# A store held back by one small scaling: average pooling with kernel 4 on one core

## Chip, core and metric

The kernel runs on one core of one Trainium2 chip. The metric is device time in microseconds (us), the time of one launch; smaller is better. The engines that work are VectorE (DVE in the profile), ScalarE (ACT), and SyncE (SP), which issues loads. Data moves between HBM and SBUF on the core's 16 DMA engines.

## The reference

```python
x: (64, 256, 8192) float32, kernel_size = 4, stride = 4
for i in range(out_len):                       # 2048
    output[:, :, i] = np.mean(x[:, :, 4*i : 4*i+4], axis=2)
```

Every four neighbouring elements are averaged. 536.87 MB are read and 134.22 MB are written; there is hardly any arithmetic per byte.

## The kernel before, in words

The input is taken as one flat array and cut into 64 blocks of 128 partitions x 16384 elements (8.39 MB). Two blocks make a run, so there are 32 runs. One block becomes 128 x 4096 results, and one run is stored by a single DMA of 128 x 8192 results (4.19 MB).

There are two input buffers, `xt[0]` for the first and `xt[1]` for the second block of a run, and two output buffers `ot[0]` and `ot[1]`, which runs use in turn. The order of the work is written by hand with semaphores. The helper `take` (lines 60 to 61) waits on an engine until a semaphore has a value and takes that value off again. For each block of a run (function `pair`, lines 91 to 112):

- VectorE waits until the block has landed (`full[k]`, line 95). For the first block it then signals `landed` (line 97) and waits until the output buffer's last store is through (line 98).
- VectorE adds neighbours in two passes (`sums`, lines 75 to 81): 8192 sums in place (line 77), then 4096 sums into the output buffer (line 79).
- SyncE waits for that (`free`, line 101), signals ScalarE (`summed`, line 102) and issues the load of the same half of the next run into the buffer that has come free (line 103, through `load`, line 64). So a second block's load is issued when the second block of the run ahead of it has been summed.
- ScalarE multiplies the 4096 sums by 1/4 in place (line 106).

When both blocks are done, ScalarE issues the run's store on its own DMA queue (line 112). It first waits until its scaling is through (`scaled`, line 109) and, in lines 110 and 111, for `landed`: the first block of the *next* run must have landed. One `landed` is taken ahead of the loop (line 118), so that the count is right.

In the profile the loads run on queue q1 and ScalarE's stores on q10. Both queues use the same 16 DMA engines. A load is 8 packets of 65,536 bytes on each engine, a store 8 of 32,768, and each is followed by a small packet that raises the semaphore.

Thirty runs go through a loop of 15 passes (line 132) with the store on ScalarE. Run 30 (line 138) uses one `tensor_reduce` per block and is stored by SyncE; run 31 (lines 142 to 157) is done in smaller pieces. Both are written out behind the loop, and neither waits for `landed` before a store.

Of the kernel before, what the change touches and what calls it, by code (L numbers as in the profile page):

```python
# [1 line left out]

# [4 lines left out]


FULL = 16384
PAIR = 2  # L10
ROUND = 2 * PAIR

TAIL = (8192, 8192)


@with_exitstack
def kernel(
    ctx: ExitStack,
    tc: tile.TileContext,
    x: bass.AP,  # L20
    kernel_size: bass.AP,
    stride: bass.AP,
    out: bass.AP,
):
    nc = tc.nc
    K, S = int(kernel_size), int(stride)
    assert K == S == 4
    B, C, L = x.shape
    assert L % K == 0
    P = nc.NUM_PARTITIONS  # L30
    dt = x.dtype
    add, mult = mybir.AluOpType.add, mybir.AluOpType.mult

    M = FULL // K
    blocks = B * C * L // P // FULL
    runs = blocks // PAIR
    assert blocks * P * FULL == B * C * L and blocks % ROUND == 0 and sum(TAIL) == FULL

    xr = x.rearrange("b c l -> (b c l)").rearrange("(n p k m) -> n k p m", p=P, k=PAIR, m=FULL)
    orun = out.rearrange("b c l -> (b c l)").rearrange("(n p m) -> n p m", p=P, m=PAIR * M)  # L40


    xt0 = ctx.enter_context(nc.sbuf_tensor([P, FULL], dt))
    xt1 = ctx.enter_context(nc.sbuf_tensor([P, FULL], dt))
    ot0 = ctx.enter_context(nc.sbuf_tensor([P, PAIR * M], dt))
    ot1 = ctx.enter_context(nc.sbuf_tensor([P, PAIR * M], dt))
    xt, ot = [xt0, xt1], [ot0, ot1]


    full = [nc.alloc_semaphore(f"full{k}") for k in range(2)]  # L50
    piece = [nc.alloc_semaphore(f"piece{k}") for k in range(len(TAIL))]
    free = nc.alloc_semaphore("free")
    summed = nc.alloc_semaphore("summed")
    landed = nc.alloc_semaphore("landed")
    summed_last = nc.alloc_semaphore("summed_last")
    scaled = nc.alloc_semaphore("scaled")
    scaled_last = nc.alloc_semaphore("scaled_last")
    stored = [nc.alloc_semaphore(f"stored{k}") for k in range(2)]

    def take(engine, sem, n):  # L60
        engine.wait_ge(sem, n).then_inc(sem, -n)  # L61

    def load(n, k):
        d = nc.sync.dma_start(out=xt[k][:, :], in_=xr[n, k])
        d.then_inc(full[k], 16)
        return d

    for k in range(2):  # L70
        tc.no_tile_sem_insts.add(load(0, k).ins.name)
    tc.close()
    tc.compile()  # L73

    def sums(t, o):
        w = t.shape[1]
        nc.vector.tensor_tensor(out=t[:, : w // 2], in0=t[:, ::2], in1=t[:, 1::2], op=add)  # L77
        nc.vector.drain()
        return nc.vector.tensor_tensor(  # L79
            out=o, in0=t[:, : w // 2 : 2], in1=t[:, 1 : w // 2 : 2], op=add  # L80
        )

    def reduce(t, o):
        return nc.vector.tensor_reduce(  # L84
            out=o,
            in_=t.rearrange("p (m k) -> p m k", k=K),
            op=add,
            axis=mybir.AxisListType.X,
        )

    def pair(n, q, ahead, store):


        for k in range(PAIR):
            take(nc.vector, full[k], 16)
            if k == 0:
                nc.vector.sem_inc(landed, 1)
                take(nc.vector, stored[q], 16)
            add_up = sums if store is nc.scalar else reduce
            add_up(xt[k][:, :], ot[q][:, k * M : (k + 1) * M]).then_inc(free, 1)  # L100
            take(nc.sync, free, 1)
            nc.sync.sem_inc(summed, 1)
            ahead(k)
            o = ot[q][:, k * M : (k + 1) * M]
            take(nc.scalar, summed, 1)
            means = nc.scalar.mul(o, o, 1.0 / K)  # L106
        done = scaled if store is nc.scalar else scaled_last
        means.then_inc(done, 1)
        take(store, done, 1)
        if store is nc.scalar:  # L110
            take(store, landed, 1)
        store.dma_start(out=orun[n], in_=ot[q][:, :]).then_inc(stored[q], 16)


    zero = nc.const_aps.tensor(0.0, [P, 1], dt)
    nc.scalar.mul(ot[0][:, :1], zero, 1.0).then_inc(stored[0], 16)  # L116
    nc.scalar.sem_inc(stored[1], 16)
    take(nc.scalar, landed, 1)

    edges = [sum(TAIL[:i]) for i in range(len(TAIL) + 1)]  # L120
    pieces = list(zip(edges[:-1], edges[1:]))
    xe, oe = xr[runs - 1, 1], orun[runs - 1]

    def ahead_of_last(k):
        if k == 0:
            load(runs - 1, 0)
        else:
            for sem, (a, b) in zip(piece, pieces):
                nc.sync.dma_start(out=xt[1][:, a:b], in_=xe[:, a:b]).then_inc(sem, 16)

    engines = (mybir.EngineType.SP, mybir.EngineType.DVE, mybir.EngineType.Activation)
    with nc.Fori(0, (runs - 2) // 2, 1, engines=engines) as r:
        for q in range(2):
            n = r * 2 + q
            pair(n, q, lambda k: load(n + 1, k), nc.scalar)


    pair(runs - 2, 0, ahead_of_last, nc.sync)

    take(nc.vector, stored[1], 16)
    take(nc.vector, full[0], 16)
    sums(xt[0][:, :], ot[1][:, :M]).then_inc(summed_last, 1)
    for k, (sem, (a, b)) in enumerate(zip(piece, pieces)):
        take(nc.vector, sem, 16)
        sums(xt[1][:, a:b], ot[1][:, M + a // K : M + b // K]).then_inc(summed_last, 1)
        if k == 0:
            take(nc.scalar, summed_last, 1)
            nc.scalar.mul(ot[1][:, :M], ot[1][:, :M], 1.0 / K)  # L150
        o = ot[1][:, M + a // K : M + b // K]
        take(nc.scalar, summed_last, 1)
        nc.scalar.mul(o, o, 1.0 / K).then_inc(scaled, 1)  # L153
        take(nc.scalar, scaled, 1)
        c = 0 if k == 0 else M + a // K
        d = M + b // K
        nc.scalar.dma_start(out=oe[:, c:d], in_=ot[1][:, c:d]).then_inc(stored[1], 16)
    take(nc.sync, stored[0], 16)
    take(nc.sync, stored[1], 16 * len(TAIL))


# [1 line left out]
_INS = ['x', 'kernel_size', 'stride']  # L163
_OUTS = [((64, 256, 2048), 'float32')]

_NUMBERS = {'kernel_size': 4, 'stride': 4}


# [26 lines left out]
```

## Time and profile before

| | us |
|---|---|
| runs shown: lowest, median, highest of 3 | 1569.22, 1570.84, 1572.13 |
| the profiled execution, its own time | 1570.5 |
| span of the profiled execution, first to last instruction | 1569.2 |
| VectorE busy | 848.0 |
| ScalarE busy | 233.1 |
| loads, median from issue to landing | 35.0 |
| ScalarE's stores, median from issue to landing | 33.4 |

The page of the profile gives for each engine the busy time, its share of the span and the count of instructions. The DMA line has one digit for each of 40 slices of the span: the busy share of the 16 DMA engines in tenths, 9 being 90% or more. A queue's row gives packets, megabytes, and the time its packets took as a share of 16 engines' span. In a table of windows each row is a stretch of time: its limits, its length, the busy time and count of DVE, ACT and POOL, the TensorE clock, the DMA share and GB/s. A packet is counted whole in the window in which it starts, so the DMA share of a short window can be a little over 1. In the timeline a row is start, duration, engine, line and operation; the brackets give how long the engine sat idle before it and what released it. A row that ends in "x3" joins three instructions, and its duration runs from the first to the last. Behind the views stand the trace's records of every single DMA packet, with start, duration, size and queue but not the number of the DMA engine.

### The profile page before, as it was taken

The numbers are of one execution on the slowest core, as the hardware profiler recorded it, in microseconds if no ns is written. First come the engines' busy times: TensorE is split into PE (matmuls) and PEld (weight loads), VectorE is DVE, ScalarE is ACT, GpSimd is POOL, SyncE is SP. The second block draws the span as 40 slices with busy tenths as digits, with TensorE's granted clock in tenths as the row PEclk, the third lists the DMA queues.
The fourth block names the chain that finished last, engine by engine and source line by source line (L and its number), as shares of the span: only waits on it lengthen the run. The fifth ranks groups of instructions, "written<-read, shape, count | busy, mean of one in ns | idle before, by whom it ended". The sixth has DMA issues, their size and how long they took to land. (4 is left out here: it accounts for less than half of the span.)

```text
span 1569.2 us, 1086 instructions
## 1 busy us (share of the span) xinstructions
DVE 848.0 (54%) x128; ACT 233.1 (15%) x67; POOL 0.2 (0%) x4
## 2 busy tenths in 40 slices
DVE  3645546545465464664646546465464664646666
ACT  1101011010110101101011010110101101011011
POOL 0000000000000000000000000000000000000000
DMA  9999999999999999999999999999999999999999
GB/s 428 412 430 438 431 438 441 416 441 428 449 426 431 431 436 418 434 440 429 429 423 417 432 428 428 417 426 434 436 441 423 419 426 435 426 424 424 434 398 388
DMA packets 14112, 671.09 MB, mean 428 GB/s; under 512 B 1568, under 2 KB 1568, under 8 KB 1568
## 3 DMA queue, kind: packets, MB, share of 16 engines
q1 hardware_dynamic: 9504, 541.07, 80.6%
q10 hardware_dynamic: 4608, 130.03, 19.2%
HBM read 536.87 MB, written 134.22 MB: 428 GB/s over the span
## 5 line engine op out<-in xcount | busy, mean ns | idle before, releaser
L77 DVE TENSOR_TENSOR xt<-xt 128x8192 f32<-128x8192 f32 (+1 forms) x63 | 539.1, 8557 | 685.6 <-DVEq L61 685.6
L106 ACT ACTIVATE ot<-ot 128x4096 f32<-128x4096 f32 x62 | 224.2, 3616 | 1300.8 <-ACTq L61 1300.8
L79 DVE TENSOR_TENSOR ot<-xt 128x4096 f32<-128x4096 f32 (+1 forms) x63 | 274.5, 4358 | 4.7
L84 DVE TENSOR_REDUCE ot<-xt 128x4096 f32<-128x16384 f32 x2 | 34.4, 17220 | 18.3 <-DVEq L61 18.3
L150 ACT ACTIVATE ot<-ot 128x4096 f32<-128x4096 f32 x1 | 3.6, 3617 | 12.8 <-ACTq L61 12.8
L153 ACT ACTIVATE ot<-ot 128x2048 f32<-128x2048 f32 x2 | 3.8, 1910 | 9.5 <-ACTq L61 9.5
L116 ACT ACT_TABLE_LOAD x1 | 1.3, 1283 | 2.4 <-PEq L73 2.4
L116 ACT ACTIVATE ot<-const-float32-0.0 128x1 f32<-128x1 f32 x1 | 0.2, 203 | 0.0
L176 POOL MEMSET const-bfloat16-1.0<- 128x1 bf16 x1 | 0.1, 102 | 0.0
L176 POOL MEMSET const-uint8-127<- 128x1 uint8 x1 | 0.1, 102 | 0.0
L176 POOL MEMSET const-float32-0.0<- 128x1 f32 x1 | 0.1, 99 | 0.2 <-issue 0.2
L176 POOL MEMSET const-float32-1.0<- 128x1 f32 x1 | 0.1, 99 | 0.0
## 6 DMA issues: line engine op xcount, KB each, us to landing
out_dram<-ot ACTq DMA_DIRECT2D x30, 4096.0 KB, 33.4
xt<-in_x_dram SPq DMA_DIRECT2D x2, 4096.0 KB, 18.4
out_dram<-ot SPq DMA_DIRECT2D x1, 4096.0 KB, 34.0
out_dram<-ot ACTq DMA_DIRECT2D x1, 3072.0 KB, 16.2
out_dram<-ot ACTq DMA_DIRECT2D x1, 1024.0 KB, 10.4
xt<-in_x_dram SPq DMA_DIRECT2D x63, 35.0
```

The costliest lines, as they stand in the source:

```text
L77: nc.vector.tensor_tensor(out=t[:, : w // 2], in0=t[:, ::2], in1=t[:, 1::2], op=add)
L79: return nc.vector.tensor_tensor(out=o, in0=t[:, : w // 2 : 2], in1=t[:, 1 : w // 2 : 2], op=add)
L84: return nc.vector.tensor_reduce(out=o, in_=t.rearrange("p (m k) -> p m k", k=K), op=add, axis=mybir.AxisListType.X,)
L106: means = nc.scalar.mul(o, o, 1.0 / K)
L116: nc.scalar.mul(ot[0][:, :1], zero, 1.0).then_inc(stored[0], 16)
L150: nc.scalar.mul(ot[1][:, :M], ot[1][:, :M], 1.0 / K)
L153: nc.scalar.mul(o, o, 1.0 / K).then_inc(scaled, 1)
L176: nc = _bacc.Bacc("TRN2", target_bir_lowering=False, num_devices=1)
```

## The change

ScalarE no longer scales the 4096 columns of a run's second block in one instruction. It scales the first 2656, waits for `landed`, then scales the last 1440 and issues the store. The wait for `landed` between the scaling and the store is gone, since it has moved ahead of the second scaling. This holds for the 30 runs of the loop. Loads, sums, the first block's scaling, run 30 and run 31 are as before.

```diff
+REST = 1440
...
             take(nc.scalar, summed, 1)
+            if k == 1 and store is nc.scalar:
+                nc.scalar.mul(o[:, :-REST], o[:, :-REST], 1.0 / K)
+                take(nc.scalar, landed, 1)
+                o = o[:, -REST:]
             means = nc.scalar.mul(o, o, 1.0 / K)
         done = scaled if store is nc.scalar else scaled_last
         means.then_inc(done, 1)
         take(store, done, 1)
-        if store is nc.scalar:
-            take(store, landed, 1)
         store.dma_start(out=orun[n], in_=ot[q][:, :]).then_inc(stored[q], 16)
```

## The prediction

> **What bounds the kernel now.** I read the page first, then the windows cut at the store issues, then the timeline of one run, then the records of single DMA packets in the trace. The page:
>
> ```profile
> span 1569.2 us, 1086 instructions
> DVE 848.0 (54%) x128; ACT 233.1 (15%) x67; POOL 0.2 (0%) x4
> DMA  9999999999999999999999999999999999999999
> q1 hardware_dynamic: 9504, 541.07, 80.6%
> q10 hardware_dynamic: 4608, 130.03, 19.2%
> ```
>
> VectorE is busy for 54% and ScalarE for 15%, while the packets of both queues fill 80.6 + 19.2 = 99.8% of the time of the 16 DMA engines. No engine is the bound: the kernel ends when the bytes are through, so a gain must come from DMA packets that take less time, and a loss from longer ones or from a queue that runs empty. The windows, one per run, from one store issue to the next (length first, GB/s last), show that runs are not alike:
>
> ```profile
> 61.60:111.89 50.29, 26.22 (x5) 7.23 (x2) 0.00 (x0) 1.00 0.99 417
> 111.89:160.33 48.44, 26.24 (x5) 7.23 (x2) 0.00 (x0) 1.00 1.00 433
> ...
> 549.37:598.05 48.68, 26.24 (x5) 7.23 (x2) 0.00 (x0) 1.00 1.01 435
> 598.05:647.07 49.02, 26.23 (x5) 7.23 (x2) 0.00 (x0) 1.00 1.00 424
> ...
> 990.26:1039.71 49.45, 26.24 (x5) 7.23 (x2) 0.00 (x0) 1.00 1.00 423
> ```
>
> VectorE and ScalarE do the same work in each (26.2 and 7.23 us), yet a run takes between 48.44 and 49.45 us. The 28 runs from 111.89 to 1479.92 take 1368.03, or 48.86 each: the first ten 48.62, the other eighteen 48.99.
>
> The packet records (start, duration, size, queue) say where this goes. A 65,536-byte load packet takes 2418 ns undisturbed, a 32,768-byte store packet 1213 ns. Per run an engine has 16, 8, and 3 of 9 ns for semaphores: 38.69 + 9.70 + 0.03 = 48.42 us, less about 0.1 for the 4 ns by which neighbours overlap: 48.3. All packets together exceed these durations by 16.6 us per engine: 0.6 before the first store, 1.2 in the first run, 0.4 in the next ten, 12.0 in the following eighteen, 0.4 just behind the last of these stores and 1.8 in the tail. Nearly all of it lies in load packets 1 to 7 us behind a store issue.
>
> Joining packets whose start is another's end (less 4 ns) gives each engine's sequence. With T the store issue, at a block's landing: the engine that landed last has started its next load packet 0.72 us before T, in every run, because the store is released by that landing. In the first ten of the 28 runs, this last engine alone pays, 0.07 to 0.48 us a run, 0.25 on average; in the first nine of them the other fifteen pay 0.003. So it falls further behind each time: from 1.3 us behind the foremost to 4. From some 4.7 us on (598 us) another thing comes in: all 16 engines stretch a packet together around T + 4 us, by about 1 us, in most of the eighteen runs. The lead then stays near 5 us, since the foremost engines find their next load not yet there.
>
> **The change, part by part.** The timeline around one store:
>
> ```profile
> 982.89 3.62 ACT L106 ACTIVATE ot<-ot 128x4096 f32<-128x4096 f32 x1 [24.89 <-ACTq L61]
> 982.98 49.80 SPq L64 DMA_DIRECT2D xt<-in_x_dram  x3
> 990.21 8.69 DVE L77 TENSOR_TENSOR xt<-xt 128x8192 f32<-128x8192 f32 x1 [7.54 <-DVEq L61]
> 990.26 0.34 ACTq L112 DMA_DIRECT2D out_dram<-ot  x1
> 998.98 4.43 DVE L79 TENSOR_TENSOR ot<-xt 128x4096 f32<-128x4096 f32 x1
> 1003.63 3.62 ACT L106 ACTIVATE ot<-ot 128x4096 f32<-128x4096 f32 x1 [17.12 <-ACTq L61]
> ```
>
> ScalarE finishes a run at 982.89 + 3.62 = 986.51 and waits for the landing until 990.2; the store goes out 0.05 us behind VectorE's start on the landed block.
>
> *Added instructions.* ScalarE's rows give 3.616 us for 4096 columns, 1.910 for 2048, 0.203 for one: 0.833 ns a column and 0.2 fixed. So 2656 columns take 2.42 us, 1440 take 1.40, together 0.2 more than the one instruction: 30 x 0.2 = 6 us of ScalarE in all, beside 1300 us idle; nothing.
>
> *The moved wait.* The first part ends at 982.89 + 2.42 = 985.3, 4.9 us ahead of the landing, so the landing still ends the wait last. Behind it now stand 1.40 us of scaling and the hand-over to the store (in the tail 1548.44 + 1.91 to the issue at 1550.46: 0.11). The store goes out some 1.5 us later, 30 times. Queued behind it on ScalarE is only the next run's first scaling, at 1003.63, 11.9 us behind the new issue; if that cover were gone, ScalarE would hand its results on late. The buffer of the store is wanted again two runs on, 2 x 48.86 = 97.7 us, and the store lands 33.4 us after its issue. SyncE's loads wait for VectorE alone: the next goes out 13.2 us behind the landing as before, and while the store is held back the engines work on the load issued at 982.98, 7.3 us ahead of it. So 1.5 us without a store are filled with load packets, and the later store costs no time by itself. If that load were not there, the price would be the whole 30 x 1.5 = 45 us.
>
> *What it moves.* A store comes between load packets of 2.42 us, so 1.5 us is more than half a packet. The last engine, 0.72 us into its packet at the issue before, will be 2.2 us into it. The trace has this position: in the first two of the 28 runs the fourteen foremost engines were 1.65 to 2.19 us past the end of the landed load, in the first packet of their next one, and paid 0.00. Engines 0.72 to 0.92 us into that same first packet paid 0.06 to 0.48; one at 1.15 paid 0.22, at 1.13 and 1.41 nothing. By these rows the last engine would stop paying. The cost of the new position is bounded by the nearest rows: from nothing (48.44 a run or a little less) to the stretch of the run at 990.26, for all runs (49.45). I take the end near nothing, since its rows have the same place in the same load, and not just the same distance. Then it does not fall behind, 4.7 us are not reached, and the common stretch stays away too.
>
> *Sum.* If all 28 runs took 48.44: 28 x (48.86 - 48.44) = 11.8. If they took the 48.62 of the first ten: 28 x 0.24 = 6.7. The first run, the start and the tail stay as they are; the store issued at 1479.92 lands by 1515, 54 us ahead of the end. The profiled execution took 1570.5 us for its span of 1569.2, as good as the median of 1570.84, so I go from 1570.5: 1558.7 to 1563.8. I take **1561**.
>
> Against the change speaks a row, then a rule. From issue to landing a store takes 33.4 us, all of which moves back. The Trainium skill, "DMA: Bandwidth & Descriptors", section "Rules for kernel authors", says to issue a DMA early and wait late, so that its fixed cost is overlapped; by it the hold is a loss. No store here is waited for within 64 us of its landing, so the trace gives the rule little to act on.
>
> **The rivals.**
> *The last engine falls behind for a reason other than the store's position* (it may simply be the slower one), or something else stretches the packets from 598 us on, such as what is read there. Then the later store is hidden beside loads and nothing moves: 1570.5, give or take 3. For it: what the stretch is made of is not in the trace, and the runs at 647 and 1039 have little of it with the same lead. Against it: the engines paying, and the onset at 4.7 us of lead, go with position.
> *The later store meets the engines worse* and the common stretch starts in the first runs. It is decided by where the foremost engines stand when the first store packet enters, at T + 4 before and about T + 5.5 after; if the stretch belongs to stores entering with 4 us of spread, it stays, and the later store also adds its packets to the next load. All 28 runs at 48.99 give 28 x 0.13 = 3.7 more, 1574; all at 49.45 give 28 x 0.59 = 16.5, 1587. For it: all 16 engines stretched in the first run already, with 0.5 us of spread, so spread is not the only condition.
> *The hold is exposed*, the rule above as a mechanism of this kernel: the foremost engines run out of loads during it and idle, 30 x 1.5 = 45, 1615. Against it: the load is issued 7.3 us ahead.
> *The last engine still pays but the lead grows more slowly*, because the second load of a run lands earlier by up to one store packet (1.2 us) and its successor is issued earlier: the late runs come later; 1565 to 1567.
> That the change does not do what it says is excluded by the listing of ScalarE's instructions: 2656 and 1440 columns stand in the loop, the store behind them.
>
> **How the numbers follow.** Forecast 0.50 (1556 to 1566); slower growth 0.08; nothing moves 0.17; worse meeting 0.23; exposed hold 0.02. A measurement of this kernel can tell about 0.2% (3.1 us) from no change. Faster: 0.50 + 0.08 = 0.58; same 0.17; slower 0.23 + 0.02 = 0.25. The likeliest one's own range is 1556 to 1566. The range that should hold 8 in 10 starts at 1555, a little under the sum with 48.3 us a run, and reaches to 1577, past no change and the milder half of the worse meeting; outside stay the common stretch in full and the exposed hold.
>
> **What would show it.** In the changed profile: the store issue 1.5 us behind VectorE's start on the landed block; runs of 48.4 to 48.6 us through to the end, also beyond 598; the page's DMA share still 99% with more GB/s; in the packet records, fewer load packets over 2418 ns behind the store issues and a last engine that stays within 2 or 3 us of the foremost. Wrong would be the step on position, if runs lengthen again although the issue has moved; wrong would be the step on cover, if DMA shares drop below 0.98 in these windows.

## The result and the profile after

The changed kernel takes **1552.85 us** (median of 4, 1552.55 to 1553.13) against 1570.82 for the kernel before on the same chip (median of 4, 1569.22 to 1572.13): ratio 0.9886, interval 0.9869 to 0.9903, so 18 us less. Its profiled execution took 1552.82 us, with a span of 1551.5. The page after:

```profile
span 1551.5 us, 1116 instructions
DVE 847.9 (55%) x128; ACT 239.2 (15%) x97; POOL 0.2 (0%) x4
q1 hardware_dynamic: 9504, 541.07, 80.6%
q10 hardware_dynamic: 4608, 130.03, 19.4%
HBM read 536.87 MB, written 134.22 MB: 433 GB/s over the span
```

The DMA engines are about as full as before (80.6 + 19.4 = 100.0% against 99.8%), the bytes and packets are the same, and ScalarE is busy for 6.1 us more. Most of the gain is not idle time removed: the same packets took 14.5 us less time on the average engine. The other 3.2 of the 17.7 us by which the span shrank are time in which the average engine had no packet, 2.9 of them behind the thirtieth store. The windows from one store issue to the next (limits, length, busy time of DVE, ACT and POOL, clock, DMA share, GB/s) show where:

```profile
63.36:112.60 49.24, 26.23 (x5) 7.43 (x3) 0.00 (x0) 1.00 1.00 426
112.60:160.93 48.33, 26.23 (x5) 7.43 (x3) 0.00 (x0) 1.00 1.00 434
...
595.95:644.30 48.35, 26.24 (x5) 7.44 (x3) 0.00 (x0) 1.00 1.00 434
...
982.64:1031.00 48.36, 26.24 (x5) 7.44 (x3) 0.00 (x0) 1.00 1.00 435
...
1417.77:1466.13 48.36, 26.23 (x5) 7.43 (x3) 0.00 (x0) 1.00 1.00 434
```

Every run behind the first takes 48.3 to 48.4 us, early and late. Before, runs took 48.44 to 49.47 and most were longer from 598 us on. The timeline of the run at 982:

```profile
981.00 1.40 ACT L111 ACTIVATE ot<-ot 128x1440 f32<-128x1440 f32 x1 [5.92 <-ACTq L62]
981.07 8.69 DVE L78 TENSOR_TENSOR xt<-xt 128x8192 f32<-128x8192 f32 x1 [8.63 <-DVEq L62]
982.64 0.34 ACTq L115 DMA_DIRECT2D out_dram<-ot  x1
```

ScalarE's second scaling starts at the landing together with VectorE, lasts the 1.40 us of the estimate, and the store goes out 1.57 us behind VectorE's start (0.05 before). VectorE waits 8.63 us ahead of it, 7.54 before: on the last engine the store takes one turn less ahead of the second block's landing, so the second half of a run is summed earlier and its buffer is loaded earlier, 8.3 us ahead of VectorE's next start instead of 7.2.

The single DMA packets: what they take beyond 2418 ns (load) and 1213 ns (store) adds up to 2.0 us per engine, against 16.6 before. 0.7 of it lies ahead of the first store, 1.0 in the first run, 0.4 in all the rest. The last engine stands 2.2 to 2.4 us past its landing at each store issue and pays nothing; the foremost is never more than 0.85 us ahead of it.

From these traces the whole difference of the spans, 17.7 us, can be laid out by stretches between store issues:

| stretch | before | after | difference |
|---|---|---|---|
| start to first store issue | 61.60 | 63.36 | +1.8 |
| first run | 50.29 | 49.24 | -1.1 |
| 28 runs | 1368.03 | 1353.53 | -14.5 |
| last of these stores to the end | 89.28 | 85.4 | -3.9 |

Of the first and last row some 1.6 us are nothing but the store issue standing later against the landings (the last engine 2.3 us past its landing instead of 0.72). What is left is +0.2 at the start and -2.3 at the end. The last row in the windows, before and after:

```profile
1479.92:1569.20 89.28, 60.87 (x8) 14.67 (x5) 0.00 (x0) 1.00 0.94 395
```

```profile
1466.10:1551.50 85.40, 59.28 (x8) 14.67 (x5) 0.00 (x0) 1.00 0.97 418
```

That 14.5 stands here twice is chance. Of the 14.5 us of packet time on the average engine, 12.1 fall in the 28 runs, 0.3 in the first run and 2.2 behind the last of these stores; a run's length follows its last engine, which paid more than the average.

### The profile page after: what moved, and what is told of

It reads as the page before. It is cut to its first block, busy times and chain, and to the rows that moved or that the text cites. A ratio compares the mean times of both kernels' runs of the same rounds, so it can differ in the third digit from the quotient of the medians.

```text
span 1551.5 us, 1116 instructions
## 1 busy us (share of the span) xinstructions
DVE 847.9 (55%) x128; ACT 239.2 (15%) x97; POOL 0.2 (0%) x4
## 3 DMA queue, kind: packets, MB, share of 16 engines
q1 hardware_dynamic: 9504, 541.07, 80.6%
q10 hardware_dynamic: 4608, 130.03, 19.4%
## 5 line engine op out<-in xcount | busy, mean ns | idle before, releaser
L111 ACT ACTIVATE ot<-ot 128x4096 f32<-128x4096 f32 (+1 forms) x62 | 157.8, 2545 | 597.4 <-ACTq L62 597.4
L108 ACT ACTIVATE ot<-ot 128x2656 f32<-128x2656 f32 x30 | 72.5, 2416 | 680.6 <-ACTq L62 680.6
L153 ACT ACTIVATE ot<-ot 128x4096 f32<-128x4096 f32 x1 | 3.6, 3617 | 13.9 <-ACTq L62 13.9
```

Of the source, the lines that this page charges most:

```text
L108: nc.scalar.mul(o[:, :-REST], o[:, :-REST], 1.0 / K)
```

## The experiments

"The last engine" is the one that finishes a landed block last, "pays" means that its packets take longer than undisturbed, and "the common stretch" is a time in which all 16 engines have a long packet. The theory on trial: an engine is slowed if the store reaches it too soon behind the end of a load; that makes one engine fall behind the others; and with the engines apart, something stretches packets on all of them. Rivals: the split of the scaling in itself; any later store being better in step; a cause that sets in at 600 us by itself.

**split_only**: the two scalings, both ahead of the wait.

```diff
+            if k == 1 and store is nc.scalar:
+                nc.scalar.mul(o[:, :-REST], o[:, :-REST], 1.0 / K)
+                o = o[:, -REST:]
             means = nc.scalar.mul(o, o, 1.0 / K)
...
             take(store, landed, 1)
```

> ScalarE scales the second block in the same two parts (2656 and 1440 columns), but both ahead of the wait for the landing, so that the store goes out where it did before, some 0.05 us behind VectorE's start. If the position of the store against the load packets is the cause: as before, 1570.8, runs of 48.9, a last engine that pays 0.25 a run, and the common stretch from some 4.7 us of lead on. If splitting the scaling is the cause, or what ScalarE does in itself: 1553.

1570.32 us, ratio 0.9988 (0.9973 to 1.0002); runs of 48.66 us in the first ten and 48.93 later; the last engine paid 0.07 to 0.63. The split does nothing.

**idle_multiply**: the delay without the split.

```diff
+            if k == 1 and store is nc.scalar:
+                means.then_inc(scaled, 1)
+                take(nc.scalar, scaled, 1)
+                take(nc.scalar, landed, 1)
+                means = nc.scalar.mul(o[:, -1440:], o[:, -1440:], 1.0)
...
-        if store is nc.scalar:
-            take(store, landed, 1)
```

> The scaling is whole and ahead of the landing; behind the landing ScalarE multiplies the last 1440 columns by 1.0, which changes no value, and then issues the store. Same 1.5 us of delay, no split, nothing left unscaled. If the position is the cause: 1553, runs of 48.34. If it matters that part of the scaling is left over: 1571.

1552.95 us, ratio 0.9886 (0.9869 to 0.9902), runs of 48.33. What ScalarE does in the 1.4 us is of no importance; the time of the store issue decides.

**rest64, rest640, rest2600, idle_5us**: other delays, with `REST` at 64, 640 and 2600, and one of about 5 us.

```diff
-REST = 1440
+REST = 64        # 640, 2600
```

> As the changed kernel, with 64 columns left over: 0.2 + 64 x 0.83 ns = 0.26 us, so the store goes out about 0.4 us later than before and the last engine is some 1.15 us into its first packet instead of 0.72. By the rows of before (0.92 paid 0.06 and 0.08; 1.15 paid 0.22; 1.13 and 1.41 paid nothing) the payment is smaller or partly gone: between 1553 and 1566. If a gain grows in step with the delay, 18 us for 1.57 us: 1566. If only 1440 columns work: 1571.

> As the changed kernel, with 2600 columns left over: 2.37 us, so the store goes out about 2.5 us later than before and the last engine is some 3.25 us past its landing, 0.8 us into its second load packet. If what counts is how far the engine is past its landing: the rows of before with 0.7 to 0.9 us in a second packet paid 0.00 to 0.02, so 1553 again. If it counts where in a packet it is, whichever packet: 0.8 pays, runs of 48.6 and later 49, 1565 to 1571. If a later store is better in step: 1540, which lies under the packets' own time, so no.

> As the changed kernel, with 640 columns left over (0.74 us): the last engine is some 1.55 us past its landing at the store issue. With 64 columns it was 1.10 us past, took the store behind its second load packet and paid every time; with 1440 and 2600 columns it took the store behind its third or fourth and paid nothing. If there is a step where the store slips behind the third packet (engines 1.4 us and more past their landing did so before): 1553, no payment. If the payment fades with the delay: about 1563.

For idle_5us, in idle_multiply:

```diff
-                means = nc.scalar.mul(o[:, -1440:], o[:, -1440:], 1.0)
+                nc.scalar.mul(o, o, 1.0)
+                f = ot[q][:, :1100]
+                means = nc.scalar.mul(f, f, 1.0)
```

> All scaling is ahead of the landing; behind it ScalarE multiplies 4096 and then 1100 columns by 1.0, so that the store goes out about 4.9 us later than before and the last engine is some 5.6 us past its landing, where the foremost engines stood when the common stretch came. If the stretch comes from engines so far past a landing when the store is issued: it comes in every run, 1571 to 1587. If it needs engines far apart from each other: 1553. If a longer hold costs time because the engines run out of loads: the DMA share falls and the time rises over 1553 by up to 28 x 3.3 = 92.

The position of the last engine at the store issue, the load packets it takes behind its landing before the store, and what it pays are from the packet records. Each ratio is against the kernel before as it ran beside that kernel on the same chip (medians 1570.8 to 1571.6):

| kernel | us past landing | load packets before the store | pays, us a run | runs, us: first ten / later | time, us (ratio, interval) |
|---|---|---|---|---|---|
| before | 0.72 | 2 | 0.25 | 48.62 / 48.99 | 1570.82 |
| rest64 | 1.10 | 2 | 0.38 | 48.73 / 49.17 | 1570.69 (0.9991, 0.9976 to 1.0007) |
| rest640 | 1.6 to 1.7 | 3 | 0.00 | 48.34 / 48.34 | 1552.73 (0.9878, 0.9862 to 0.9895) |
| changed | 2.2 to 2.4 | 3 | 0.00 | 48.34 / 48.34 | 1552.85 (0.9886, 0.9869 to 0.9903) |
| rest2600 | 3.2 to 3.3 | 3 (once 4) | 0.00 | 48.33 / 48.33 | 1552.86 (0.9885, 0.9868 to 0.9901) |
| idle_5us | 5.5 to 5.6 | 4 | 0.03 | 48.34 / 48.37 | 1553.30 (0.9882, 0.9865 to 0.9898) |

It is a step, not a slope. I had expected 64 columns to bring part of the gain; they bring none, and in the profiled execution (1574.41 us, of ten from 1563.59 to 1575.18) the payment is rather larger. At 640 columns the whole gain is there, and four more microseconds of hold add nothing to it and cost 0.6 us (1553.30 against 1552.73). The two windows beside each other, rest64 first, then rest640:

```profile
599.13:648.20 49.07, 26.24 (x5) 7.43 (x3) 0.00 (x0) 1.00 1.00 425
```

```profile
595.21:643.52 48.31, 26.23 (x5) 7.43 (x3) 0.00 (x0) 1.00 1.00 434
```

Both have the DMA share at 1.00; only GB/s and the length tell them apart. idle_5us also says that standing 5 to 6 us past a landing is harmless if the engines stand together.

**half_packets**: the kernel before, each load as two DMAs of 8192 columns.

```diff
-        d = nc.sync.dma_start(out=xt[k][:, :], in_=xr[n, k])
...
+        h = FULL // 2
...
+        for c in (0, h):
+            d = nc.sync.dma_start(out=xt[k][:, c : c + h], in_=xr[n, k][:, c : c + h])
+            d.then_inc(full[k], 16)
...
-            take(nc.vector, full[k], 16)
+            take(nc.vector, full[k], 32)
```

> The kernel before, with each load issued as two DMAs of 8192 columns: 32,768-byte packets of 1.21 us, two DMAs into the same buffer. The store goes out at the landing, 0.72 us into the last engine's next packet, as before. If the time since the landing decides: the last engine pays, falls behind, and the time is near 1571. If it decides how many load packets the engine takes before the store (two pay, three don't): the store comes behind the third or fourth half packet, nobody pays, and runs take 48.4 (8 more packets' overheads and one more semaphore packet per load, below 0.1 us): about 1555.

1559.16 us, ratio 0.9929 (0.9909 to 0.9949), with the store at the landing as before:

```profile
111.32:159.81 48.49, 26.24 (x5) 7.23 (x2) 0.00 (x0) 1.00 1.00 432
...
984.32:1032.82 48.50, 26.23 (x5) 7.23 (x2) 0.00 (x0) 1.00 1.00 432
```

The last engine stands 0.8 to 0.9 us past its landing, in which position it paid before; its store comes behind four or five half packets, and in these 28 runs no packet of any engine is more than 14 ns over its time. The runs stay at 48.5. So the time since the landing does not decide by itself. The packets are also half as long here, so that the count of load packets ahead of the store is the simplest reading, not a proof. At 48.50 a run is 0.16 longer than in the changed kernel, more than I had allowed for.

**late_second_load**: the kernel before, with a slower sum of the second block.

```diff
-            add_up = sums if store is nc.scalar else reduce
+            add_up = sums if store is nc.scalar and k == 0 else reduce
```

> The kernel before, with the store at the landing, but VectorE sums the second block of each run with one tensor_reduce: 17.2 us instead of 13.1, so that each second load is issued 4.1 us later, some 3.2 us ahead of the landing instead of 7.3. The foremost engines then can't run ahead of the last by more than about 1 to 1.5 us, since they find no load. If the common stretch needs a lead of 4 to 5 us, as the explanation has it: the last engine still pays 0.25 a run, the stretch does not come, runs of 48.6 throughout, about 1562 to 1565, faster than before with a slower VectorE. If the stretch has another cause that begins at 600 us: 1571. If engines that find no load cost time: over 1571.

1603.55 us, ratio 1.0202 (1.0181 to 1.0222). My forecast failed, and with it a part of the theory: the stretch does not need a lead of 4 to 5 us. Here the engines are within 2.5 us of each other when a first block lands, and the stretch came in every run, about 0.6 to 1.1 us wherever two engines or more had waited for their load. The timeline shows the squeeze:

```profile
690.64 17.22 DVE L84 TENSOR_REDUCE ot<-xt 128x4096 f32<-128x16384 f32 x1 [15.30 <-DVEq L61]
708.08 3.62 ACT L106 ACTIVATE ot<-ot 128x4096 f32<-128x4096 f32 x1 [28.90 <-ACTq L61]
708.17 99.64 SPq L64 DMA_DIRECT2D xt<-in_x_dram  x5
711.36 8.69 DVE L77 TENSOR_TENSOR xt<-xt 128x8192 f32<-128x8192 f32 x1 [3.50 <-DVEq L61]
```

The load is issued 3.2 us ahead of VectorE's next start. In the packet records 13 of 16 engines on average wait at the first packet behind the landed load: they have no packet for a while, or that first packet takes longer than 2418 ns. That led to a second form of the theory: the stretch comes when engines have run dry.

**hold_and_dry and hold_not_dry**: the changed kernel, with its good store position, and the second load issued later. hold_and_dry has the edit just shown; hold_not_dry this:

```diff
-            add_up(xt[k][:, :], ot[q][:, k * M : (k + 1) * M]).then_inc(free, 1)
+            if store is nc.scalar and k == 1:
+                c = 12288
+                reduce(xt[k][:, :c], ot[q][:, M : M + c // K])
+                sums(xt[k][:, c:], ot[q][:, M + c // K : 2 * M]).then_inc(free, 1)
+            else:
+                add_up(xt[k][:, :], ot[q][:, k * M : (k + 1) * M]).then_inc(free, 1)
```

> The changed kernel, with the store 1.57 us behind the landing, and VectorE sums the second block with one tensor_reduce (17.2 us instead of 13.1), so that the second load is issued 3.2 us ahead of the landing. A load's packets begin some 2 us behind its issue, and the foremost engine is through some 1.4 us ahead of the landing: it finds no load, by a few tenths of a us. If engines that run dry are what brings the common stretch: it comes in every run although the store's position is good and the engines are close together, about 1590 to 1605. If the stretch needs a bad position of the store, or a lead of 4 us: 1553 to 1558.

> As hold_and_dry, but VectorE uses tensor_reduce on 12288 columns of the second block and the two passes on the other 4096: about 16.2 us instead of 13.1, the load goes out 4.2 us ahead of the landing and its packets begin some 2.2 us ahead, before the foremost engine is through (1.4 to 1.6). If running dry brings the stretch: none here, 1553, a step of some 40 us against hold_and_dry for 1 us of VectorE. If the slower VectorE costs in step: three quarters of what hold_and_dry costs.

1577.92 us (ratio 1.0033, 1.0010 to 1.0056) against 1557.37 (0.9919, 0.9899 to 0.9940). First hold_and_dry, then hold_not_dry:

```profile
164.77:214.43 49.66, 30.33 (x4) 7.43 (x3) 0.00 (x0) 1.00 1.00 422
...
1000.89:1049.99 49.10, 30.34 (x4) 7.44 (x3) 0.00 (x0) 1.00 1.00 427
```

```profile
114.72:164.79 50.07, 29.49 (x6) 7.43 (x3) 0.00 (x0) 1.00 1.00 420
164.79:213.12 48.33, 29.50 (x6) 7.43 (x3) 0.00 (x0) 1.00 1.00 434
...
1035.16:1083.50 48.34, 29.49 (x6) 7.43 (x3) 0.00 (x0) 1.00 1.00 434
```

VectorE is 0.84 us a run slower in the first (30.33 against 29.49), and the time differs by 20 us. Both forecasts missed, 1590 to 1605 and 1553, and the step fell short of my 40. One reason is that I had reckoned the 3.2 and 4.2 us from late_second_load. The changed kernel issues its second load a microsecond earlier to begin with, and the timelines have it 4.4 us (hold_and_dry) and 5.1 us (hold_not_dry) ahead of VectorE's next start, on average; in hold_and_dry only some 3 to 5 engines a run wait, not 13. hold_not_dry begins with two bad runs, in the first of which all 16 engines waited, has one more of 48.70, and otherwise keeps to 48.3, although VectorE works 3.3 us a run longer than in the changed kernel (29.49 against 26.23).

This table counts, for each store behind the first run, how many engines had waited for their first load packet just ahead of it (called dry), and gives the mean stretch per engine behind the store issue. Stores with exactly one dry engine are left out:

| kernel | no engine dry | two or more dry |
|---|---|---|
| before | 13 stores, 0.09 us | 9 stores, 0.90 us |
| changed, rest640, idle_5us | 84 stores, 0.00 to 0.01 | none |
| hold_and_dry | 6 stores, 0.36 | 17 stores, 0.87 |
| hold_not_dry | 24 stores, 0.01 | 1 store, 1.61 |
| late_second_load | 2 stores, 0.42 | 26 stores, 0.87 |
| no_hold, below | 8 stores, 0.50 | 19 stores, 0.95 |
| rest64 | 16 stores, 0.15 | 10 stores, 1.08 |
| split_only | 18 stores, 0.19 | 5 stores, 0.71 |

The table leans on one reading: a first packet over 2418 ns counts as a wait, and that it is one is not shown. If only pauses count in which an engine had no packet for 50 ns or more, two or more engines are dry ahead of 3 stores in the kernel before, 5 in hold_and_dry, 6 in no_hold and 23 in late_second_load, and 18 stores of hold_and_dry without any such pause still have 0.62 us. That loads which come too late bring the stretch is shown by hold_and_dry against hold_not_dry; that it takes engines without a packet is not.

**no_hold**: the kernel before without the wait for the landing.

```diff
-                nc.vector.sem_inc(landed, 1)
...
-        if store is nc.scalar:
-            take(store, landed, 1)
...
-    take(nc.scalar, landed, 1)
```

> The kernel before without the wait for the landing: the store goes out as soon as the run is scaled, some 3.7 us ahead of the landing, when the engines are in the seventh of the load's eight packets. If a store is only bad within some 1.4 us behind a landing: 1553, and the hold was never needed. If it is bad wherever the load in progress is about to end: over 1571. A third way: the store takes its turns ahead of the last load packets, so that the landing comes later, VectorE gives its buffer back later and the engines run dry: 1590 and more.

1580.32 us, ratio 1.0064 (1.0034 to 1.0094), nearest to "over 1571". The third way has a part in it: by the table's count 2 engines or more were dry ahead of 19 of 28 stores. But stores with no dry engine are slow too (0.50), so what an early store meets is not resolved.

**early_first_store**: does the stretch of the first run belong to the first store?

```diff
+    zeros = nc.const_aps.tensor(0.0, [P, 128], dt)
-    nc.scalar.mul(ot[0][:, :1], zero, 1.0).then_inc(stored[0], 16)
+    nc.scalar.mul(ot[0][:, :128], zeros, 1.0).then_inc(scaled, 1)
+    take(nc.scalar, scaled, 1)
+    nc.scalar.dma_start(out=orun[0][:, :128], in_=ot[0][:, :128]).then_inc(stored[0], 16)
```

> The changed kernel, and ahead of the loop ScalarE stores 128 x 128 zeros into the first run's output, which that run's own store writes over later. In all kernels so far the first run alone has a stretch of about 1 us at its store. If that belongs to the first store that ScalarE's queue issues or to the first write: it goes to the start, where it costs little, and the first run takes 48.3 to 48.5; 1552. If it belongs to engines that are all within 0.7 us of each other, or to the place in the program: as the changed kernel, 1552.9.

1554.54 us, ratio 0.9890 (0.9873 to 0.9906): 1.7 more than the changed kernel, so neither expectation held to the number. The first run's last engine still pays 0.90. So it isn't a matter of the queue's first store or the first write, at least not of a small one. The cause of the stretch in the first run stays open.

## Why the prediction was right and wrong

*What bounds the kernel*: right in the main. The DMA share stayed at 100%, and of the 17.7 us by which the span shrank 14.5 are packet time on the average engine (16.55 - 2.03). That a gain "must come from DMA packets that take less time" left out the other 3.2, time without a packet, nearly all of it at the end of the program.

*Added instructions, the moved wait*: right. 6.1 us more of ScalarE against 6; the store 1.52 us later (from 0.05 to 1.57) against 1.5, hidden beside loads: idle_5us hides 4.9 us as well. A hold of 4.9 us costs 0.6 us over one of 0.9, so the exposed hold falls. The rule of the Trainium skill, "DMA: Bandwidth & Descriptors", section "Rules for kernel authors", to issue early and wait late, goes the other way than the times here: 1580 us for the earliest store, 1571 at the landing, 1553 from 0.9 us behind it.

*What it moves*: right in its outcome. The last engine stopped paying, the lead stayed under 0.85 us, and behind the first run the common stretch stayed away to the end. The measure was too loose. By distances, rows at 1.13 us that paid nothing stood beside rows at 1.15 that paid; rest64 pays at 1.10 every time, and half_packets does not at 0.8. Behind the first run, the count of load packets ahead of the store, two or three, sorts the last engine's payments in the kernels of the first table; the distance does not. It does not sort every engine's: the engine at 1.15 that paid 0.22 took the store behind its third packet. And the lead of 4.7 us (by the landings at 598 it is 4.2) is not what starts the stretch: late_second_load has the stretch with engines 2.5 us apart. The prediction had the right fact beside it, "the foremost engines find their next load not yet there", but took it for what limits the lead, not for the source of the stretch.

*Sum*: this is where it failed. Two terms were too small:

- "The first run, the start and the tail stay as they are." This term was put at nothing and was 3.2 us: 1.1 in the first run and 2.3 at the end, less 0.2 at the start. The reason given, that the last of these stores lands 54 us ahead of the end, does not see that both stages hold what the loop holds. In the first run of the kernel before, two engines took the store behind their second load packet and were slowed twice, one by 2.0 and one by 2.3 us in all, the other fourteen by 0.95 to 1.25. In the changed kernel all 16 took it behind their third and lost 1.2 at most. At the end, the load of the last block was issued 3.1 us ahead of VectorE's next start, and after the change 4.2 us ahead, before first, then after:

```profile
1525.28 0.82 SPq L129 DMA_DIRECT2D xt<-in_x_dram  x2
...
1528.42 8.69 DVE L77 TENSOR_TENSOR xt<-xt 128x8192 f32<-128x8192 f32 x1 [3.31 <-DVEq L61]
```

```profile
1508.46 0.82 SPq L132 DMA_DIRECT2D xt<-in_x_dram  x2
...
1512.70 8.69 DVE L78 TENSOR_TENSOR xt<-xt 128x8192 f32<-128x8192 f32 x1 [4.40 <-DVEq L62]
```

  Before, 15 of the 16 engines then had no packet for 1.5 to 2.7 us, after the change none. The engine that finished the loads last had 2.5 us of long packets behind the thirtieth store, and has 0.2. The other kernels fall the same way: where this load goes out 3.2 us ahead or less (split_only, rest64, late_second_load, half_packets, no_hold), packets from that issue to the end are 1.8 to 1.9 us over their time on the average engine; where it goes out 4.2 or more ahead, 0.2 at most, but for hold_and_dry with 0.7.
- "If all 28 runs took 48.44". That was the best run seen, and itself held a payment of the last engine (about 0.1 in that run). The packets' own sum, worked out a few lines above it as 48.3, was the right term: 48.34 measured, 28 x (48.86 - 48.34) = 14.5 instead of 11.8. From there I also took 1561, half way to the sum for a last engine that goes on paying as in the first ten runs, although the step before had argued that it stops.

With both terms the sum is 1570.5 - 14.5 - 3.2 = 1552.8. The lower end of 1555 came from runs of 48.3 with everything else unchanged; with the second term alone put right the sum is 1556.0. So it is the term for the ends of the program, put at nothing, that takes the time below the range.

*The rivals*: "nothing moves" fell with idle_multiply, since the store's position alone brings the gain. "The later store meets the engines worse" fell with four delays, all good from 0.9 to 4.9 us. "The last engine still pays but the lead grows more slowly" fell with the packet records: it pays nothing. What happens inside the engines stays open: no run shows why a packet grows longer, only when.

## What to carry to other kernels

When the DMA engines are full from start to end, compare packet durations between stages that move the same bytes: a share of 100% hides packets that take a third longer, and only GB/s and the length of the stage show it. Where one DMA is released by the landing of another, move its issue by a fraction of a packet in both directions and look for a step. Take the floor for a sum from the packets' own undisturbed time, not from the best stage seen, and if the state of the engines changes, let it change at the ends of the program too.

## What was not expected of the hardware

A store issued at a landing reached the last engine behind its second load packet, and that engine lost 0.25 us a run; with the store behind the third, it lost nothing. The step lies between 1.10 and 1.6 us past the landing with packets of 65,536 bytes; with 32,768 there was no such payment at 0.8.

The long packet is mostly the one just ahead of the store. Around the first 29 stores of the kernel before, the load packets are 13.4 us over their undisturbed time on the average engine. 10.1 us of this lie in the load packet that an engine carries right ahead of its first store packet, and 2.0 in the one right behind that store packet. The store's own packets keep to 1213 ns (1228 at most). So the time is lost mostly before the store's first packet starts on that engine.

Where loads come so late that two or more engines wait for them (0.05 to 2.0 us), a stretch of 0.9 us on average follows at the next store, and on all 16 engines, those that had work included. What passes between them is not in the traces. Such waits aren't the only way to it: the first run has a stretch in every kernel, one store of the kernel before had 0.60 without a dry engine, and no_hold 0.50 on average.
